# Where two DRAM sums of the down weights are formed, and the order of work at the change from up to down, in an encoder block on one core

## Chip, cores and metric

The kernel runs on one core of one Trainium2 chip. The metric is the device time of one execution in microseconds; the time before is the median of three runs. Names of engines: PE is TensorE, DVE is VectorE, ACT is ScalarE, POOL is GpSimd, SP is SyncE, which here only issues transfers.

## What is computed

One layer of an encoder: 512 positions, 1024 features, 4096 hidden features, all in float32. Cut to its outline:

```python
n = rms_norm(h, norm_mix_pre)
z_gmlp, q, k, v, gates = split(n @ w_in)                 # 1024 x 7680
y_a = gmlp_spatial_gating(gelu(z_gmlp), ...)             # 512 wide
y_b = dilated window attention of q, k, v                # 512 wide
g_a, g_b = sigmoid(gates + b_gate)
merged = g_a * (y_a @ w_branch_a) + g_b * (y_b @ w_branch_b)
h = h + rms_norm(merged @ w_out, norm_mix_post)
n2 = rms_norm(h, norm_mlp_pre)
hid = square(relu(n2 @ w_up))                            # 1024 -> 4096
h = h + rms_norm(hid @ w_down, norm_mlp_post)            # 4096 -> 1024
```

The change touches the gates (in one place), the product with `w_up`, called up here, and the product with `w_down`, called down.

## The kernel before

Every float32 operand of a matmul is split in two parts, a high one (a copy by ScalarE into the matmul's format) and a low one (VectorE subtracts the high part from the operand), and each product is three matmuls: high by high, high by low, low by high. So for each operand that TensorE reads, ScalarE and VectorE have one operation each, one after the other.

The stages follow each other: norm and projections, attention, the gMLP branch, the gates with the two branch products, `w_out`, up, down.

**Gates** (`seven_pairs`, `gate_weights`, `gate_evac`, `branches`). Seven groups i = 0 to 6 of 256 gate columns. Each loads 1 MB of `w_in` into tile `gw` (two transfers on SP) and the branch weights `bw`, forms sums of quarter blocks on VectorE (line 331 is the first), splits them and runs seven half-size products of Strassen's kind (line 345) and the branch products (lines 84 to 86, tile `pf`).

**Up** (line 1000 on). The first four tiles of 128 hidden columns are plain products. Then i runs from 2 to 15, a group being 256 hidden columns. `prep` loads 1 MB of `w_up` into tile `upw` (`raw_up`, line 930, pool `wback`, tag `raw`, two buffers), forms four sums (line 970 is the first) and splits them; the high and low parts `hl` share five buffers. Seven products follow, numbered 6, 1, 5, 2, 7, 3 and 4 in the order of the code (line 995), 12 matmuls each. Product 4 of a group stands in `tail`, which is called in the next group behind product 6; its join (line 1035) and the Relu of the pair (line 1037) follow, and the Square (line 1018) in the next group. The first half of the second column tile, `c1`, is ready after product 2 (line 1023).

**Down** (line 1040 on). The 4096 hidden features are four groups c = 0 to 3 of 1024 (`hid`), and the product is one level of Strassen's scheme with seven products, each over four groups: X with activations a11, Z with a12, Y with a21, W with a12 plus a sum, X again with s2, Z with a11 plus a sum, Y with a22. A group of a product (`run`, lines 1081 to 1083, tile `pd`) is 24 matmuls of 128 by 512 columns, with one split of its activations (`h_split`, tile `hhl`) and two splits of its weights (`w_split`, tile `hl`). The weights of the first, second and fourth product come straight from `w_down` (`block`, line 1057, tile `dnw`, the same two `raw` buffers as up's loads). The other three need sums of weight blocks:

- `t1d` in DRAM, for the sixth product: two blocks added, read at line 1062.
- `t3d` in DRAM, for the third product: two blocks added; line 1116 loads it into SBUF (`tsum`, and `tend` for the last group), and `add_block` (line 1111) then adds further blocks in place for the fifth and the seventh product.

Both DRAM sums are formed by transfers from DRAM to DRAM on POOL's queue (`form_next`, line 736): per sum and group c a copy of 1 MB, then an accumulating transfer of 1 MB, which waits until its copy has landed. The list `forming` gives the order. `form_next` ties a transfer to a place in the program by a one-element copy on POOL out of a tile that was just written; what is issued after it follows in POOL's order. Whoever writes that tile again waits for this copy: in up that is the Relu of the same pair.

**What sets the order.** The code order is only a start: a scheduler moves instructions on each engine, and `tc.issue_after(x)` holds what stands under it behind x. The engines then run their lists in order. SP's list holds all loads of weights, so a load that waits for its buffer holds those behind it. In down, `h_split` is held behind `late`, two results of the last group but one of up; the weight splits are not held.

Of the kernel before, what the change touches and what calls it, by code (L numbers as in the profile page):

```python
# [10 lines left out]
F32 = mybir.dt.float32  # L11
F32R = mybir.dt.float32r
AF = mybir.ActivationFunctionType
ALU = mybir.AluOpType
# [22 lines left out]
def block_kernel(ctx: ExitStack, tc: tile.TileContext, x, norm_mix_pre, w_in, b_gate, ln_v_gain, ln_v_bias,  # L37
# [40 lines left out]
    def split_into(hi, lo, src, sub=nc.vector):  # L78
        nc.scalar.activation(hi, src, AF.Copy)  # L79
        return sub.tensor_tensor(lo, src, hi.bitcast(F32), op=ALU.subtract)  # L80
# [610 lines left out]
    for g2 in range(2):  # L691
        raw = wload([KD, 2 * P], lambda r: [(r, fcols(w_in, COL_U + g2 * 2 * P, KD, 2 * P))], "uw")
        for j in range(2):
# [15 lines left out]
            for c in range(4):  # L709
# [19 lines left out]
    w7 = w_down.rearrange("(c j h p) d -> c h p j d", p=P, h=2, j=4)  # L729
    halves = [slice(0, 512), slice(512, 1024)]  # L730
    t1d, t3d = [tc.dram_tile([4, P, 4, 512], F32, name=nm) for nm in ("t1d", "t3d")]
    forming = [(t, c, *part) for t, parts in ((t1d, ((0, 0, None), (0, 1, ALU.add))), (t3d, ((0, 1, None), (1, 1, ALU.add))))
               for c in range(4) for part in parts]

    def form_next(seen, n=1):
        ins = nc.gpsimd.tensor_copy(warm[:1, :1], seen)
        with tc.issue_after(ins.ins):
            for _ in range(n):
                t, c, h, hf, op = forming.pop(0)
                nc.gpsimd.dma_start(t[c], w7[c, h, :, :, halves[hf]], **({"accum_op": op} if op else {}))  # L740
# [22 lines left out]
    def gate_evac(i, dst, X):  # L763
        d = i + GSTD
        nc.scalar.activation(dst, X, AF.Sigmoid, bias=cols[:, d:d + 1])
        if i < 6:
            form_next(dst[:1, :1], 2 if i < 2 else 1)

    def gate_after(i):
        d = i + GSTD  # L770
# [220 lines left out]
    def product(n, ps, w, first):  # L991
        (wh, wl), (bh, bl) = w[n], moving[n]
        for j in range(KH):
            for m, (a, b) in enumerate(((wh, bh), (wh, bl), (wl, bh))):
                nc.tensor.matmul(ps, a[:, j], b[:, j], start=first and not (j or m), stop=(j == KH - 1 and m == 2), skip_group_check=True)  # L995

    def half_bank(tag):
        return psB.tile([P, 512], F32, name="p" + tag, tag=tag, bufs=4)[:, :256]
# [5 lines left out]
    for i in range(NSTD, KF // 2):  # L1004
        f = 2 * i
        if f % 8 == 0:
            hid.append((hida if f < 24 else hidb).tile([P, 8, S], F32, name="hid"))
        c2, c1 = hid_of(f), hid_of(f + 1)
        w = prep(i)
        Y, Z, X = half_bank("acc"), half_bank("acc"), half_bank("tp")  # L1010
        product(6, Y, w, True)
        both = tail()[1] if tail else None
        product(1, X, w, True)
        p1, z5, u2, u3 = snap("p1", 2), snap("z5"), snap("u2"), snap("u3")
        taken = nc.scalar.activation(p1, X, AF.Copy)
        if both is not None:
            with tc.issue_after(taken.ins):
                nc.scalar.activation(both, both, AF.Square)
        joins[i] = nc.vector.tensor_tensor(u2, Y, p1, op=ALU.add)
        product(5, Z, w, True)  # L1020
        nc.scalar.activation(z5, Z, AF.Copy)
        product(2, X, w, False)
        done = nc.scalar.activation(c1[:, :256], X, AF.Copy)
        if i > NSTD + 1 and forming:
            form_next(c1[:1, :1])
        product(7, Y, w, False)
        nc.vector.scalar_tensor_tensor(u3, Y, -1.0, p1, op0=ALU.mult, op1=ALU.subtract)
        product(3, Z, w, False)
        nc.vector.tensor_tensor(c1[:, 256:], Z, u2, op=ALU.add)
        ins = nc.vector.tensor_tensor(c2[:, 256:], u3, z5, op=ALU.subtract)  # L1030
        late = late if i == KF // 2 - 1 else (done, ins)

        def tail(w=w, Y=Y, p1=p1, c2=c2, f=f):
            product(4, Y, w, False)
            joined = nc.vector.scalar_tensor_tensor(c2[:, :256], Y, -1.0, p1, op0=ALU.mult, op1=ALU.subtract)
            both = hid[f // 8][:, f % 8:f % 8 + 2]
            nc.scalar.activation(both, both, AF.Relu)
            return joined, both
    joined, both = tail()
    up.close()  # L1040

    dpool = pool(dn, "dpool", bufs=3)
# [11 lines left out]

    def block(c, h, hf):
        raw = raw_down()
        nc.sync.dma_start(raw, w7[c, h, :, :, halves[hf]])
        return raw

    def formed(c):  # L1060
        raw = raw_down()
# [6 lines left out]
    def h_split(src, first=False):  # L1068
        hl = (d0pool if first else dpool).tile([P, 2, 4, 256], F32R, name="hhl", tag="hhl")
        with tc.issue_after(late[0].ins), tc.issue_after(late[1].ins):  # L1070
            lows.append(split_into(hl[:, 0], hl[:, 1], src))
        return hl[:, 0], hl[:, 1]

    lows = []

    def w_split(parts):
        return [split_back(part, [2, 512]) for part in parts]
# [16 lines left out]
    a11, a12, a21, a22 = [[b[:, :, h, z * 256:z * 256 + 256] for b in blk] for z in range(2) for h in range(2)]  # L1094

    for c in range(NC):
        run(X, c, True, h_split(a11[c], c == 0), w_split(pairs(block(c, 0, 0))))
        if c == 1:
            nc.scalar.activation(both, both, AF.Square)
    big = sumpool.tile([P, 4 * NC - 4, 512], F32, name="tsum")  # L1100
# [10 lines left out]
            nc.gpsimd.dma_start(part, w7[c, h, :, js, halves[hf]], accum_op=ALU.add)  # L1111

    s2 = []
    for c in range(NC):
        for part, js in each_part(c):
            nc.sync.dma_start(part, t3d[c, :, js])

    def first_sums(c, after):
        with tc.issue_after(after.ins):
# [5 lines left out]
    first_sums(1, lows[3])  # L1125
    for c in range(NC):
        run(Z, c, True, h_split(a12[c]), w_split(pairs(block(c, 1, 0))))
        if c in (1, 2):
            first_sums(c + 1, lows[-1])

# [129 lines left out]
```

## Time and profile before

| | us |
|---|---|
| three runs | 1096.55, 788.82, 791.18 |
| their median | 791.18 |
| the profiled execution | 794.81 |
| its span, from the first to the last instruction | 793.0 |
| TensorE busy in the span | 775.2 |
| VectorE, ScalarE, GpSimd busy | 603.0, 461.4, 92.4 |
| mean granted TensorE clock in the span | 0.993 |
| transfers: SP's queue, POOL's queue | 83.50 MB, 43.61 MB |

The page's times are of the one profiled execution, in us from the first instruction; a group's row gives the line, the engine, the operation, tiles written and read, size, count, busy time and the mean of one in ns. A wait is put down to what ended it. In this execution the gates run from about 297 to 418, `w_out` to 477, up to 633, down to the end.

### The profile page before, as it was taken

What the parts mean: (1) busy time and instruction counts of PE and PEld (TensorE: products, weight loads), DVE (VectorE), ACT (ScalarE), POOL (GpSimd) and SP (SyncE); (2) the same over time, 40 slices, a digit from 0 to 9 for tenths busy, and PEclk for the clock granted to TensorE, in tenths of its full rate; (3) what the DMA queues carried; (4) which work ended last, traced back from release to release, by engine and by line L of the source; (5) the groups of instructions that cost most, each with busy time, mean ns of one, the idle gap of its engine ahead of it and who ended that gap; (6) DMA issues with size and microseconds to landing.
All of it is one profiled execution on the core that took longest, in us unless ns stands there. A gap on an engine that the chain in (4) does not pass through costs nothing.

```text
span 793.0 us, 12277 instructions
## 1 busy us (share of the span) xinstructions
PE 775.2 (98%) x4821; PEld 696.6 (88%) x4821; DVE 603.0 (76%) x963; ACT 461.4 (58%) x747; POOL 92.4 (12%) x125
## 2 busy tenths in 40 slices
PE   9999999999999999979999999999999989999996
PEld 6888999999988889979998899999999868888885
DVE  6884688979665977758756569998888688968885
ACT  6351467978776454435444557566666565665671
POOL 2310200010105200100110210001110000202010
PEclk9999999999999999989999999999999999999999
DMA  9733734353616324877674521449873774979802
GB/s 311 237 113 115 204 100 107 86 155 104 189 53 180 99 80 118 229 186 164 204 205 133 197 102 59 157 131 243 214 210 112 264 289 163 181 236 206 227 0 107
DMA packets 104748, 128.29 MB, mean 162 GB/s; under 512 B 3265, under 2 KB 75233, under 8 KB 103794
## 3 DMA queue, kind: packets, MB, share of 16 engines
q1 hardware_dynamic: 83920, 83.50, 33.4%
q0 software_dynamic: 20480, 43.61, 23.0%
q8 instruction: 38, 0.62, 0.3%
q10 hardware_dynamic: 290, 0.40, 0.1%
q14 instruction: 20, 0.16, 0.1%
HBM read 117.53 MB, written 26.74 MB: 182 GB/s over the span
## 4 chain that ended last, share of the span: by engine, by line
PE 88%; DMA 5%; DVE 3%; ACT 2%; issue 1%; POOL 0%; SPq 0%; POOLq 0%; DVEq 0%; ACTq 0%
PE pacc L995 10%; PE pg L345 10%; PE pd L1081 6%; PE pd L1083 6%; PE pd L1082 6%; PE pgacc L345 6%; PE pf L86 5%; PE pf L85 5%; PE pf L84 5%; PE ptp L995 4%; PE pv L84 3%; PE pv L85 3%; PE pv L86 3%; PE pgS L345 2%; PE pd L84 2%; PE pd L86 2%
## 5 line engine op out<-in xcount | busy, mean ns | idle before, releaser
L1081 PE MATMUL pd<-hl,hhl 128*128 128x512 f32 x224 | 87.5, 392 | 4.5 <-ACT hhl L79 4.5
L1082 PE MATMUL pd<-hl,hhl 128*128 128x512 f32 x224 | 87.9, 392 | 0.0
L1083 PE MATMUL pd<-hl,hhl 128*128 128x512 f32 x224 | 87.4, 392 | 0.0
L995 PE MATMUL pacc<-nt,hl 128*128 128x256 f32 x504 | 67.1, 280 | 0.0
L995 PEld LDWEIGHTS pacc<-nt,hl 128*128 128x128 f32 x504 | 62.6, 188 | 0.1
L1081 PEld LDWEIGHTS pd<-hl,hhl 128*128 128x128 f32 x224 | 42.4, 190 | 13.4 <-ACT hhl L79 4.8
L74 ACT ACTIVATE hi<-s 128x1024 fp32r<-128x1024 f32 x30 | 31.7, 1059 | 36.7 <-DVE s L332 13.4
L1083 PEld LDWEIGHTS pd<-hl,hhl 128*128 128x128 f32 x224 | 42.4, 189 | 9.0
L1082 PEld LDWEIGHTS pd<-hl,hhl 128*128 128x128 f32 x224 | 42.3, 189 | 8.9
L80 DVE TENSOR_TENSOR hl<-dnw,hl 128x1024 fp32r<-128x1024 f32 x32 | 38.5, 1221 | 9.6 <-ACT hl L79 9.6
L75 DVE TENSOR_TENSOR lo<-s,hi 128x1024 fp32r<-128x1024 f32 x30 | 36.6, 1223 | 11.1 <-ACT hi L74 11.0
L79 ACT ACTIVATE hl<-s 128x1024 fp32r<-128x1024 f32 x28 | 29.4, 1058 | 26.8 <-DVE s L978 18.2
L995 PE MATMUL pacc<-n,hl 128*128 128x256 f32 x336 | 44.8, 279 | 0.0
L79 ACT ACTIVATE hl<-dnw 128x1024 fp32r<-128x1024 f32 x32 | 33.7, 1057 | 19.0 <-PE pd L1083 9.1
L84 PE MATMUL pf<-nh,hi 128*128 128x512 f32 x112 | 44.3, 396 | 0.0
L86 PE MATMUL pf<-nh,lo 128*128 128x512 f32 x112 | 44.1, 393 | 0.0
L85 PE MATMUL pf<-nl,hi 128*128 128x512 f32 x112 | 44.0, 393 | 0.0
L995 PEld LDWEIGHTS pacc<-n,hl 128*128 128x128 f32 x336 | 41.9, 188 | 0.1
L79 ACT ACTIVATE hhl<-hid 128x1024 fp32r<-128x1024 f32 x24 | 25.3, 1058 | 25.1 <-PE pd L1083 25.0
L80 DVE TENSOR_TENSOR hhl<-hid,hhl 128x1024 fp32r<-128x1024 f32 x24 | 29.3, 1222 | 13.6 <-ACT hhl L79 13.3
L80 DVE TENSOR_TENSOR hl<-s,hl 128x1024 fp32r<-128x1024 f32 x28 | 34.2, 1222 | 6.2 <-ACT hl L79 6.1
L85 PE MATMUL pv<-lo,nh 128*128 128x512 f32 x96 | 37.6, 392 | 0.0
(383 smaller groups left out, 2278.5 us busy)
## 6 DMA issues: line engine op xcount, KB each, us to landing
upw<-in_w_up_dram SPq DMA_DIRECT2D x16, 1024.0 KB, 5.6
qkw<-in_w_in_dram SPq DMA_DIRECT2D x24, 512.0 KB, 5.2
dnw<-in_w_down_dram SPq DMA_DIRECT2D x12, 1024.0 KB, 5.3
gw<-in_w_in_dram SPq DMA_DIRECT2D x16, 512.0 KB, 5.8
t1d<-in_w_down_dram POOLq DMA_DIRECT2D x8, 1024.0 KB, 9.0
t3d<-in_w_down_dram POOLq DMA_DIRECT2D x8, 1024.0 KB, 9.1
slab<-in_w_in_dram SPq DMA_DIRECT2D x6, 1024.0 KB, 10.2
tsum<-in_w_down_dram POOLq DMA_DIRECT2D x6, 1024.0 KB, 9.5
```

The lines of the kernel that those rows point to most:

```text
L74: nc.scalar.activation(hi, raw, AF.Copy)
L75: (sub or nc.vector).tensor_tensor(lo, raw, hi.bitcast(F32), op=ALU.subtract)
L79: nc.scalar.activation(hi, src, AF.Copy)
L80: return sub.tensor_tensor(lo, src, hi.bitcast(F32), op=ALU.subtract)
L84: nc.tensor.matmul(ps, ah, bh, start=start, stop=False)
L85: nc.tensor.matmul(ps, ah, bl, start=False, stop=False)
L86: return nc.tensor.matmul(ps, al, bh, start=False, stop=stop)
L345: nc.tensor.matmul(ps, a[:, j], b[:, j], start=first and not (j or i), stop=(j == KH - 1 and i == 2), skip_group_check=True)
L995: nc.tensor.matmul(ps, a[:, j], b[:, j], start=first and not (j or m), stop=(j == KH - 1 and m == 2), skip_group_check=True)
L1081: nc.tensor.matmul(ps, ah, bh, start=start, stop=False, skip_group_check=True)
L1082: nc.tensor.matmul(ps, ah, bl, start=False, stop=False, skip_group_check=True)
L1083: return nc.tensor.matmul(ps, al, bh, start=False, stop=stop, skip_group_check=True)
```

## The change

Four things:

1. `forming` is turned round: t3d first, then t1d. In the gates nothing is formed any more. In up, groups 4 to 15 form all 16 transfers, two each in groups 6, 8, 10 and 12, one in the others. Before, the gates' first six groups formed the eight for t1d (2, 2, 1, 1, 1, 1) and groups 4 to 11 of up the eight for t3d.
2. The first down product's first group is held behind the last matmul of up's last product (`turned`).
3. In the first down product, the load and the weight splits of groups 2 and 3 are held behind both operations of the activations' split of the same group; `h_split` is written out for this, with its two operations in lists.
4. The loads of t3d into SBUF stand one behind each weight load of the second product, instead of ahead of that product.

```diff
-    forming = [(t, c, *part) for t, parts in ((t1d, ((0, 0, None), (0, 1, ALU.add))), (t3d, ((0, 1, None), (1, 1, ALU.add))))
+    forming = [(t, c, *part) for t, parts in ((t3d, ((0, 1, None), (1, 1, ALU.add))), (t1d, ((0, 0, None), (0, 1, ALU.add))))
                for c in range(4) for part in parts]
...
         nc.scalar.activation(dst, X, AF.Sigmoid, bias=cols[:, d:d + 1])
-        if i < 6:
-            form_next(dst[:1, :1], 2 if i < 2 else 1)
...
-                nc.tensor.matmul(ps, a[:, j], b[:, j], start=first and not (j or m), stop=(j == KH - 1 and m == 2), skip_group_check=True)
+                ins = nc.tensor.matmul(ps, a[:, j], b[:, j], start=first and not (j or m), stop=(j == KH - 1 and m == 2), skip_group_check=True)
+        return ins
...
-        if i > NSTD + 1 and forming:
-            form_next(c1[:1, :1])
+        if i > NSTD + 1:
+            form_next(c1[:1, :1], 2 if i in (6, 8, 10, 12) else 1)
...
-            product(4, Y, w, False)
+            turned = product(4, Y, w, False)
...
-            return joined, both
-    joined, both = tail()
+            return joined, both, turned
+    joined, both, turned = tail()
...
-        nc.sync.dma_start(raw, w7[c, h, :, :, halves[hf]])
+        loads.append(nc.sync.dma_start(raw, w7[c, h, :, :, halves[hf]]))
...
-            lows.append(split_into(hl[:, 0], hl[:, 1], src))
+            his.append(nc.scalar.activation(hl[:, 0], src, AF.Copy))
+            lows.append(nc.vector.tensor_tensor(hl[:, 1], src, hl[:, 0].bitcast(F32), op=ALU.subtract))
...
     for c in range(NC):
-        run(X, c, True, h_split(a11[c], c == 0), w_split(pairs(block(c, 0, 0))))
+        h = h_split(a11[c], c == 0)
+        with ExitStack() as order:
+            if c > 1:
+                order.enter_context(tc.issue_after(his[-1].ins))
+                order.enter_context(tc.issue_after(lows[-1].ins))
+            w = w_split(pairs(block(c, 0, 0)))
+        with nullcontext() if c else tc.issue_after(turned.ins):
+            run(X, c, True, h, w)
...
-    for c in range(NC):
-        for part, js in each_part(c):
-            nc.sync.dma_start(part, t3d[c, :, js])
...
         run(Z, c, True, h_split(a12[c]), w_split(pairs(block(c, 1, 0))))
+        for part, js in each_part(c):
+            with tc.issue_after(loads[-1].ins):
+                nc.sync.dma_start(part, t3d[c, :, js])
```

What this makes of the engines' lists is shown at three places. ScalarE where up ends: `p`, `z` and `hid` out of PSUM are up's last group, line 1037 is the Relu of the last pair and line 1099 its Square; `hl<-dnw` are weight splits of the first down product, two per group, `hhl<-hid` its activation splits. Before:

```order
L1021 ACTIVATE z_6836<-pacc 128x256
L79 ACTIVATE hl<-dnw 128x1024
L1018 ACTIVATE hid<-hid 128x1024
L79 ACTIVATE hl<-dnw 128x1024
L1023 ACTIVATE hid<-ptp 128x256
L79 ACTIVATE hl<-dnw 128x1024 x3
L1037 ACTIVATE hid<-hid 128x1024
L79 ACTIVATE hhl<-hid 128x1024 x2
L1099 ACTIVATE hid<-hid 128x1024
```

Now (lines 1020, 1017, 1022, 1036 and 1108 are the old 1021, 1018, 1023, 1037 and 1099; 1072 is the activation split's own line):

```order
L1020 ACTIVATE z_6832<-pacc 128x256
L79 ACTIVATE hl<-dnw 128x1024
L1017 ACTIVATE hid<-hid 128x1024
L1022 ACTIVATE hid<-ptp 128x256
L79 ACTIVATE hl<-dnw 128x1024
L1036 ACTIVATE hid<-hid 128x1024
L1072 ACTIVATE hhl<-hid 128x1024 x2
L79 ACTIVATE hl<-dnw 128x1024
L1108 ACTIVATE hid<-hid 128x1024
```

The three weight splits ahead of the Relu, the last of which is the fourth group's, have become one, the second group's; the others stand behind the activations. On TensorE, in the same stretch, 14 of the first group's 24 matmuls `pd` stood between up's products 5 and 2 and ten more ahead of product 4; now all 24 stand behind product 4, in one piece, and up's products 5, 2, 3, 7 and 4 follow each other directly.

POOL in up, `hid` being the tile that was just written; before, the last two of eight triggers:

```order
L736 COPY warm<-hid 1x1
L740 DMA t3d<-in_w_down_dram 512x1x512
L736 COPY warm<-hid 1x1
L740 DMA t3d<-in_w_down_dram 512x1x512
L1045 DMA gain_6918<-in_norm_mlp_post_dram 128x1024
```

Now, from the seventh trigger (group 10) on:

```order
L736 COPY warm<-hid 1x1
L740 DMA t1d<-in_w_down_dram 512x1x512 x2
L736 COPY warm<-hid 1x1
L740 DMA t1d<-in_w_down_dram 512x1x512
L736 COPY warm<-hid 1x1
L740 DMA t1d<-in_w_down_dram 512x1x512 x2
L736 COPY warm<-hid 1x1
L740 DMA t1d<-in_w_down_dram 512x1x512
L736 COPY warm<-hid 1x1
L740 DMA t1d<-in_w_down_dram 512x1x512
L1044 DMA gain_6916<-in_norm_mlp_post_dram 128x1024
L736 COPY warm<-hid 1x1
```

Each one-element copy now stands behind up to two transfers of the group before, and the last one behind the load of the norm's gain.

SP at the start of down, before:

```order
L1057 DMA dnw<-in_w_down_dram 128x4x512 x2
L1116 DMA tend<-t3d 128x1024
L1057 DMA dnw<-in_w_down_dram 128x4x512
L1116 DMA tend<-t3d 128x1024
L1057 DMA dnw<-in_w_down_dram 128x4x512
L1116 DMA tsum<-t3d 128x2048 x3
L1057 DMA dnw<-in_w_down_dram 128x4x512 x8
```

Now:

```order
L1056 DMA dnw<-in_w_down_dram 128x4x512 x5
L1136 DMA tsum<-t3d 128x2048
L1056 DMA dnw<-in_w_down_dram 128x4x512
L1136 DMA tsum<-t3d 128x2048
L1056 DMA dnw<-in_w_down_dram 128x4x512
L1136 DMA tsum<-t3d 128x2048
L1056 DMA dnw<-in_w_down_dram 128x4x512
L1136 DMA tend<-t3d 128x1024 x2
L1056 DMA dnw<-in_w_down_dram 128x4x512 x4
```

The five loads of t3d, which stood among and behind the first product's weight loads, each follow a weight load of the second product.

More of the change, by code (lines that the diff above doesn't have):

```diff
@@ L1056, in block @@
         raw = raw_down()
-        nc.sync.dma_start(raw, w7[c, h, :, :, halves[hf]])
+        loads.append(nc.sync.dma_start(raw, w7[c, h, :, :, halves[hf]]))
         return raw
+    loads = []
     def formed(c):
@@ L1070, in h_split @@
         with tc.issue_after(late[0].ins), tc.issue_after(late[1].ins):
-            lows.append(split_into(hl[:, 0], hl[:, 1], src))
+            his.append(nc.scalar.activation(hl[:, 0], src, AF.Copy))
+            lows.append(nc.vector.tensor_tensor(hl[:, 1], src, hl[:, 0].bitcast(F32), op=ALU.subtract))
         return hl[:, 0], hl[:, 1]
-    lows = []
+    his, lows = [], []
     def w_split(parts):
```

## The prediction

> **What bounds the kernel now.** I read the page's first part, then TensorE's waits, then stretches around each wait.
>
> ```profile
> PE 775.2 (98%) x4821; PEld 696.6 (88%) x4821; DVE 603.0 (76%) x963; ACT 461.4 (58%) x747; POOL 92.4 (12%) x125
> ```
> ```profile
> PE pd L1081 <- ACT hhl L79: 4.5, 1, 4.5
> PE pgacc L345 <- DVE u L365: 4.0, 1, 4.0
> ```
>
> TensorE is the bound: of the 793.0 us span it is idle in 17.8. So whatever the change does to transfers or to other engines counts only where it makes or ends an idle stretch of TensorE. Two waits in the middle make up nearly half of the idle time. In the stretches below the columns are length, busy time (instructions) of TensorE, of its weight loads, of VectorE, ScalarE and GpSimd, then granted clock, DMA share, GB/s.
>
> ```profile
> 348.65:352.69 4.04, 0.01 (x1) 0.01 (x1) 2.22 (x4) 0.00 (x0) 0.00 (x0) 0.83 0.58 193
> 352.69:358.16 5.47, 5.47 (x21) 5.08 (x22) 5.21 (x10) 3.96 (x6) 0.00 (x0) 0.50 0.00 0
> 633.23:637.78 4.55, 0.00 (x1) 0.01 (x1) 2.54 (x4) 3.01 (x4) 0.00 (x0) 1.00 1.02 424
> 638.06:641.47 3.41, 3.41 (x9) 2.62 (x9) 3.41 (x4) 2.62 (x3) 0.00 (x0) 0.50 1.00 409
> 0.00:20.00 20.00, 18.15 (x61) 12.97 (x62) 12.83 (x25) 12.92 (x29) 5.48 (x15) 1.00 0.94 312
> 780.00:793.00 13.00, 6.53 (x29) 5.07 (x27) 4.48 (x9) 1.37 (x4) 1.10 (x2) 0.95 0.29 105
> ```
>
> After each of the two waits the granted clock is 0.50: for 5.47 us of matmuls behind the first, for 3.41 behind the second. Half of that is lost as well: 2.7 and 1.7. So the wait in the gate stage costs 4.0 + 2.7 = 6.8, the wait between up and down 4.55 + 1.7 = 6.3. The other idle time is the start (1.85) and the tail (6.5), which the change does not touch.
>
> The **gate wait**, from the chain that ended last, the issues, and the page's median for such a load:
>
> ```profile
> 337.37 12.98 DMA gw<-in_w_in_dram
> 350.47 1.23 DVE s L331
> 352.69 2.93 PE pgacc L345 x12
> ```
> ```profile
> 335.24 1.18 POOL L740 DMA_DIRECT2D t1d<-in_w_down_dram  x1 [7.19 <-DMA t1d<-in_w_down_dram]
> 336.96 1.65 SPq L66 DMA_DIRECT2D gw<-in_w_in_dram  x2
> 342.50 0.67 POOL L740 DMA_DIRECT2D t1d<-in_w_down_dram  x1
> ```
> ```profile
> gw<-in_w_in_dram SPq DMA_DIRECT2D x16, 512.0 KB, 5.8
> ```
>
> A gate group's weights took 13.0 us to land where 5.8 is the median, between an accumulating transfer into t1d and the next copy. VectorE stood at its first sum until 350.47, and the join that frees TensorE's bank is queued behind that sum.
>
> The **wait between up and down**, by the timeline and the chain:
>
> ```profile
> 631.67 1.56 PE L995 MATMUL pacc<-n,hl 128*128 128x256 f32 x12
> 634.10 0.42 DVE L1035 SCALAR_TENSOR_TENSOR hid<-pacc,p 128x256 f32<-128x256 f32 x1
> 634.77 1.06 ACT L79 ACTIVATE hl<-dnw 128x1024 fp32r<-128x1024 f32 x1 [1.85 <-DMA dnw<-in_w_down_dram]
> 635.74 1.04 ACT L1037 ACTIVATE hid<-hid 128x1024 f32<-128x1024 f32 x1
> 636.68 1.04 ACT L79 ACTIVATE hhl<-hid 128x1024 fp32r<-128x1024 f32 x1
> 637.78 0.58 PE L1081 MATMUL pd<-hl,hhl 128*128 128x512 f32 x1 [4.55 <-ACT hhl L79]
> ```
> ```profile
> 627.26 7.43 DMA dnw<-in_w_down_dram
> ```
>
> Up's last product ends at 633.2. The second group's activations can be split only after its join and the Relu, and these stood behind a weight split for the fourth group, which waited for a load issued at 627.26. Meanwhile TensorE had nothing left: the first group's 24 matmuls had been run between up's last products.
>
> **The change, part by part.** Gates: eight transfers leave POOL's queue; what was late falls to the usual load time. Counted from the issue at 336.96, 5.8 us gives 342.8 instead of 350.35, and TensorE ran dry only at 348.65. Take away 6.8. Nothing else is removed there: each dropped one-element copy ran on POOL, which is 12% busy.
>
> Junction: the first group's matmuls now stand behind up's last one. Their price in TensorE's time is zero; they fill the hole. Pace of both kinds, from full stretches:
>
> ```profile
> L80 DVE TENSOR_TENSOR hhl<-hid,hhl 128x1024 fp32r<-128x1024 f32 x24 | 29.3, 1222 | 13.6 <-ACT hhl L79 13.3
> ```
> ```profile
> 660.00:680.00 20.00, 20.00 (x90) 16.57 (x89) 17.62 (x17) 12.05 (x13) 2.61 (x2) 1.00 0.60 162
> 600.00:620.00 20.00, 20.00 (x172) 20.00 (x172) 16.18 (x22) 13.63 (x19) 0.00 (x0) 1.00 0.31 106
> ```
>
> 20/90 gives 0.22 us per down matmul, 24 of them 5.3. So up ends 5.3 earlier, at 627.9, and the second group is wanted at 633.2. Its chain after 627.9: join 0.42 and Relu 1.04, high half 1.04, low half 1.22 (mean of such a subtraction), with some 0.5 of handing over: ready at 632.1 to 632.5. That fits by about 0.9. The third and fourth groups' weight splits now stand behind their activations, so no load holds ScalarE ahead of the Relu. Take away 6.3; if the 0.9 is overdrawn, some tenths come back, without a clock loss.
>
> Everything after it comes 4.6 to 6.3 us earlier, and then loads are late next. The second product's first load goes out when the third group's second weight split is done: six operations of 1.22 stand on VectorE from 631.2 on, so 638.5. It is wanted three groups after 633.2, at 649.1, and 2.3 before for its own split: it may take 8.3 us.
>
> ```profile
> 628.17 1.36 SPq L1116 DMA_DIRECT2D tsum<-t3d  x3
> ```
> ```profile
> tsum<-t3d SPq DMA_DIRECT2D x3, 1024.0 KB, 11.7
> ```
> ```profile
> DMA to landing us min/median/max: 4.8/6.0/11.1
> DMA to landing us min/median/max: 5.4/5.6/9.6
> DMA to landing us min/median/max: 3.9/5.8/13.0
> ```
>
> The last three are the landings of the tiles dnw, upw and gw, in this order. The 11.1 was the load behind the three t3d transfers, which now follow it on SP; but a t1d transfer may still run beside it. Between 6.0 (no cost) and 11.1 (2.7, plus 1.7 of clock at worst) I take 1, nearer to the median since the three are gone. The t3d transfers, now put one behind each load of the second product, go out from 639 to 656; at 11.7 each they are there by 668, and the third product wants them from 633.2 + 8 x 5.3 = 676 on: nothing.
>
> Up: eight more forming transfers in the same twelve groups, POOL's queue twice blocked per pair. The present load of this stage:
>
> ```profile
> 527.00:597.00 70.00, 70.00 (x597) 70.00 (x596) 60.09 (x86) 46.01 (x66) 11.45 (x14) 1.00 0.86 218
> ```
> ```profile
> L740 POOL DMA_DIRECT2D t3d<-in_w_down_dram x8: 645/806/1203, 510.9 to 587.6; - x8
> L1062 SPq DMA_DIRECT2D dnw<-t1d x4: 319/329/339, 705.5 to 742.7; - x4
> ```
> ```profile
> 583.99 0.37 SPq L930 DMA_DIRECT2D upw<-in_w_up_dram  x1
> 595.51 1.22 DVE L970 TENSOR_TENSOR s<-upw 128x1024 f32<-128x1024 f32 x1
> 603.97 10.08 SPq L1057 DMA_DIRECT2D dnw<-in_w_down_dram  x2
> 545.95 0.40 POOL L736 COPY warm<-hid 1x1 f32<-1x1 f32 x1 [7.32 <-ACT hid L1023]
> 552.93 1.04 ACT L1037 ACTIVATE hid<-hid 128x1024 f32<-128x1024 f32 x1
> ```
>
> From 600 to 620 two loads (603.97 and the next) at share 0.31 are 3.1 us of all DMA engines each. In 70 us at 0.86 are seven forming transfers (all but the first) and about seven loads: (60 - 22)/7 = 5.4 each. From the third trigger to the end of up, some 90 us, there will be 13 of them and nine loads: 70 + 28 = 98. So the queue is full, and the forming runs some 8 us behind. Its own readers don't mind: t3d, formed first, is read from 639 on, t1d from 705.5. A load does: it is used 11.5 us after its issue (583.99 to 595.51), so up to 11.5 costs nothing. The worst load of this stage, 9.6, already stood between two forming transfers. I take 0; the upper bound, at gw's 13.0, is (13.0 - 11.5)/2 x 10 groups = 7.5, since each buffer serves every second group. A gain is excluded, TensorE being full there.
>
> [...]
>
> POOL's queue: an accumulating transfer waits for its copy, and the next group's one-element copy stands behind it. The Relu (L1037) waits for that copy: 552.93 against 545.95, 7 us of room. POOL's waits before a second transfer were up to 7.19; a full DMA queue adds a few. I take 0; above it, ScalarE's delays of some 3 us, four times, 12 at the most if none is absorbed.
>
> **Sum.** 793.0 - 6.8 - 6.3 + 1 = 780.9 of span. The profiled execution took 794.8, so 782.7 by its clock; it is 3.6 above the median of the runs shown, 791.18, and part of its waits may be its own. On the median I take off 11.7: **779.5**.
>
> **Rivals.** (1) The wait between up and down only moves: the second product's first loads come late, since all groups start 5 us earlier. For it: 11.1 us for one of them, the last t1d transfer beside it. Against: t3d is behind them on SP. 2.7 for each of two groups and 1.7 of clock instead of my 1: 786.
>
> (2) Slower: up's loads starve. The sixteen transfers keep the queue full from the third trigger on, and every load takes more than 11.5 us. Each us beyond costs 0.5 per group, 5 in ten groups. The gain is used up from 13.9 us on; at 15.5 a load the cost is 20 us: 799.5. For it: 98 us of work for 90, gw's 13.0. Against: 9.6 as the longest in this stage, and such a load used half-KB rows and shared its queue with three others.
>
> (3) POOL's blocked queue holds the Relu four times: 12 us, 791.5, no change. For it: 7.19 against 7 us of room. Against: only that one of POOL's waits was as long, and only what goes beyond the 7 holds ScalarE.
>
> (4) The gate change does nothing: gw was late because it was itself issued late, at 336.96. Then 6.8 stay: 786.3. Against: 13.0 from issue to landing is counted after the issue.
>
> [...]
>
> **How the numbers follow.** The forecast has 0.60, rival (1) 0.17, (2) 0.10, (3) 0.05, (4) 0.08. Its own spread, with the scatter of the runs, is 775 to 784. To leave out no more than two in ten, the range goes over (1), (4) and part of (3): **774 to 790**. Two per cent, about what a measurement of this kernel can tell from no change, is 15.8 us. The waits that can go are worth 13.1, so faster by more than that needs luck in the runs: 0.10. Slower by more than that needs loads beyond 17 us: 0.04. Within: 0.86.
>
> **What would show it.** Right: no wait of TensorE at L345 in the gates and granted clock 1.00 there; gw landing below 8; pd's first 24 matmuls in one piece, a wait before the 25th below 1 us; TensorE full through up with DMA share near 1; upw landing at 7 to 10. Wrong: a wait of TensorE in up on VectorE's sums or ScalarE's splits (rivals 2 and 3), the Relu held by POOL's copy, or a wait on hl or hhl around the second product's first groups (rival 1). The sum is wrong if the total of TensorE's idle time is not 9 to 11 us.

## The result, and the profile after

The changed kernel takes 782.17 us (median of nine runs, 780.58 to 786.94), the kernel before beside it 791.54: ratio 0.9896, 95% interval 0.9867 to 0.9925. It is about 1% faster: the interval does not reach 1, and the change stays inside the two per cent that the prediction held most likely. The ratio is taken over the executions and not from the two medians, whose quotient is 0.988; one execution of the kernel before, at 1096.55, was in a slower state and is left out of it. The forecast was 779.5 in a range of 774 to 790. The profiled execution took 782.17 with a span of 780.3; before it was 793.0.

The page's first part, of the changed kernel:

```profile
PE 771.0 (99%) x4821; PEld 693.4 (89%) x4821; DVE 602.5 (77%) x963; ACT 460.6 (59%) x747; POOL 90.8 (12%) x123
```

TensorE is idle in 780.3 - 771.0 = 9.3 us of the span, where it was 17.8. Its waits, all of the changed kernel:

```profile
PE idle L159 <- DVE onesq L59: 1.1, 1, 1.1
PE pt L186 <- DVE xn L182: 0.7, 1, 0.7
PE pacc L993 <- DVE u L1026: 0.5, 1, 0.5
PE pd L84 <- DVE gs L372: 0.5, 1, 0.5
PE ptp L993 <- ACT hl L79: 0.2, 1, 0.2
```

Both long waits are gone, the one at L345 in the gates and the one on `hhl` between up and down. A small one is new: up's last product (4) now runs directly behind product 7, on the same PSUM bank, and waits 0.5 for the join that reads it. Stretches of the changed kernel, columns as before (gates, up, the junction):

```profile
337.00:353.00 16.00, 16.00 (x115) 15.02 (x114) 12.79 (x21) 7.97 (x14) 0.00 (x0) 1.00 0.43 112
527.00:597.00 70.00, 70.00 (x597) 70.00 (x596) 59.54 (x87) 46.04 (x65) 14.63 (x18) 1.00 0.95 255
620.00:634.00 14.00, 14.00 (x68) 11.79 (x68) 10.83 (x11) 9.88 (x11) 1.19 (x1) 1.00 1.06 306
```

The granted clock is 1.00 in all three, TensorE is busy throughout, and up's DMA share went from 0.86 to 0.95. What ScalarE does at the junction, in the changed kernel:

```profile
622.03 1.06 ACT L1036 ACTIVATE hid<-hid 128x1024 f32<-128x1024 f32 x1 [1.69 <-DVE hid L1034]
623.00 1.99 ACT L1072 ACTIVATE hhl<-hid 128x1024 fp32r<-128x1024 f32 x2
627.30 1.06 ACT L79 ACTIVATE hl<-dnw 128x1024 fp32r<-128x1024 f32 x1 [2.31 <-DMA dnw<-in_w_down_dram]
```

The Relu (L1036) now waits only for its own join. The third group's weight split still waits 2.31 for its load, but behind the activations, where nobody needs it yet. The landings of the tiles upw and dnw, in this order, in the changed kernel:

```profile
DMA to landing us min/median/max: 5.4/5.6/12.0
DMA to landing us min/median/max: 4.7/7.4/13.5
```

Both maxima rose (9.6 and 11.1 before). The loads did get later; in this execution TensorE did not wait for them.

### The profile page after: what moved, and what is told of

It reads as the page before. It is cut to its first block, busy times and chain, and to the rows that moved or that the text cites. A ratio compares the mean times of both kernels' runs of the same rounds, so it can differ in the third digit from the quotient of the medians.

```text
span 780.3 us, 12276 instructions
## 1 busy us (share of the span) xinstructions
PE 771.0 (99%) x4821; PEld 693.4 (89%) x4821; DVE 602.5 (77%) x963; ACT 460.6 (59%) x747; POOL 90.8 (12%) x123
## 4 chain that ended last, share of the span: by engine, by line
PE 95%; DMA 2%; ACT 1%; issue 0%; DVE 0%; POOL 0%; POOLq 0%; DVEq 0%; ACTq 0%
PE pacc L993 11%; PE pg L345 10%; PE pd L1083 6%; PE pd L1084 6%; PE pd L1085 6%; PE pgacc L345 6%; PE pf L85 5%; PE pf L84 5%; PE pf L86 5%; PE ptp L993 5%; PE pv L84 4%; PE pv L86 4%; PE pv L85 4%; PE pgS L345 3%; PE pd L84 2%; PE pd L86 2%
## 5 line engine op out<-in xcount | busy, mean ns | idle before, releaser
L1084 PE MATMUL pd<-hl,hhl 128*128 128x512 f32 x224 | 87.1, 389 | 0.0
L1085 PE MATMUL pd<-hl,hhl 128*128 128x512 f32 x224 | 87.0, 389 | 0.0
L1083 PE MATMUL pd<-hl,hhl 128*128 128x512 f32 x224 | 85.3, 390 | 0.0
L86 PE MATMUL pv<-hi,nl 128*128 128x512 f32 x96 | 37.3, 392 | 0.0
L84 PE MATMUL pv<-hi,nh 128*128 128x512 f32 x96 | 36.9, 392 | 0.0
```

The lines of the kernel that those rows point to most:

```text
L84: nc.tensor.matmul(ps, ah, bh, start=start, stop=False)
L86: return nc.tensor.matmul(ps, al, bh, start=False, stop=stop)
L1083: nc.tensor.matmul(ps, ah, bh, start=start, stop=False, skip_group_check=True)
L1084: nc.tensor.matmul(ps, ah, bl, start=False, stop=False, skip_group_check=True)
L1085: return nc.tensor.matmul(ps, al, bh, start=False, stop=stop, skip_group_check=True)
```

## Experiments

Twelve kernels ran, the changed one twice. The table gives each one's median and its ratio to the kernel before in the same job (kernels that ran side by side). "Parts" are the four points of the section on the change: 1 the forming in up alone, 2 the first group behind up, 3 the weight loads and splits behind the activations, 4 the loads of t3d behind those of the second product.

| kernel | parts | median us | ratio, 95% interval |
|---|---|---|---|
| changed | 1 2 3 4 | 782.17 | 0.9896 (0.9867 to 0.9925) |
| changed, again | 1 2 3 4 | 781.90 | 0.9880 (0.9834 to 0.9926) |
| forming only | 1 | 796.4 | 1.0059 (1.0035 to 1.0082) |
| forming put back | 2 3 4 | 785.35 | 0.9912 (0.9879 to 0.9945) |
| junction only | 2 3 | 786.32 | 0.9902 (0.9866 to 0.9939) |
| first group free | 1 3 4 | 784.97 | 0.9914 (0.9881 to 0.9947) |
| splits free | 1 2 4 | 788.37 | 0.9950 (0.9926 to 0.9973) |
| t3d loads first | 1 2 3 | 794.87 | 1.0036 (1.0015 to 1.0058) |
| no t1d | 1 2 3 4, half of the forming | 781.10 | 0.9854 (0.9824 to 0.9884) |
| one each | 2 3 4, forming spread | 780.64 | 0.9845 (0.9815 to 0.9874) |
| one each, turned | the same, product order | 780.31 | 0.9830 (0.9798 to 0.9863) |
| extra copies, tied to nothing | 1 2 3 4, 12 MB more at the start | 788.95 | 0.9958 (0.9933 to 0.9983) |
| extra copies in up | 1 2 3 4, 12 MB more | 807.71 | 1.0182 (1.0144 to 1.0220) |

The medians of the kernel before in the four jobs were 791.5, 791.7, 792.5 and 794.4, so kernels of different jobs are compared by ratio.

### Forming alone

The kernel before with part 1 alone:

```diff
-    forming = [... t1d ..., ... t3d ...]
+    forming = [... t3d ..., ... t1d ...]
...
-        if i < 6:
-            form_next(dst[:1, :1], 2 if i < 2 else 1)
...
-        if i > NSTD + 1 and forming:
-            form_next(c1[:1, :1])
+        if i > NSTD + 1:
+            form_next(c1[:1, :1], 2 if i in (6, 8, 10, 12) else 1)
```

> The kernel before with the forming alone moved (t3d first, all 16 transfers in up, none in the gates); the order at the end of up and the t3d loads are as before. Theory A (two separate waits: t1d's transfers delay a gate load, the order of work delays the second down group): the gate wait is gone with its clock loss, 4.0 + 2.7 = 6.8 us, and the wait behind up stays at 4.5 us or grows, since the down loads now run beside the last t1d transfers: 785 us, ratio 0.991. Rival B (the gate load was late because it was issued late): the gate wait stays, 791, ratio 1.00. Rival C (forming all 16 in up takes back what the gates give): gate wait gone, waits of TensorE in up, 788 to 792.

It came out slower than before, ratio 1.0059. TensorE's longest wait in it, the stretch of that wait and the one behind it, and ScalarE's rows ahead of the Relu (L1035):

```profile
PE pd L1079 <- ACT hhl L79: 12.9, 1, 12.9
```
```profile
624.77:637.67 12.90, 0.01 (x1) 0.00 (x0) 3.94 (x5) 5.00 (x6) 1.19 (x1) 0.61 1.04 357
637.67:651.32 13.65, 13.65 (x53) 11.11 (x54) 12.66 (x11) 7.80 (x8) 0.00 (x0) 0.87 0.83 270
```
```profile
628.56 2.00 ACT L79 ACTIVATE hl<-dnw 128x1024 fp32r<-128x1024 f32 x2 [9.86 <-DMA dnw<-in_w_down_dram]
634.67 1.06 ACT L79 ACTIVATE hl<-dnw 128x1024 fp32r<-128x1024 f32 x1 [4.11 <-DMA dnw<-in_w_down_dram]
635.63 1.04 ACT L1035 ACTIVATE hid<-hid 128x1024 f32<-128x1024 f32 x1
```

The gate wait is gone, but the wait between up and down grew from 4.55 to 12.9, with 13.65 x (1 - 0.87) = 1.8 of clock behind it. ScalarE stood 9.86 and 4.11 us in weight splits ahead of the Relu, waiting for loads that now run beside t1d's transfers. So part 1 moves the contention from the gates to the junction, and the junction as it was cannot stand it. None of the three theories had the time: theory A allowed that the wait grows, but not by more than the gates give.

### Forming put back, and the junction alone

The changed kernel with part 1 undone (the diff above, reversed), and the kernel before with parts 2 and 3 alone:

> The changed kernel with the forming put back (t1d in the gates, t3d in up), the rest as changed. Theory A: the gate wait of 4.0 us and its clock loss are as before, the wait behind up is gone: 791.5 - 6.3 = 785 us, ratio 0.992, and no t1d transfer beside the first down loads. Rival C: with up free of the moved transfers this one is as fast as the whole change or faster, below 782.

> The kernel before with parts 2 and 3 of the change alone (first group behind up, weight loads and splits of groups 2 and 3 held behind the activations): forming as before, loads of t3d ahead of the second product as before. In SP's list the fourth group's load then stands behind all five loads of t3d, 4 MB at 3.1 us each. Theory A (the 12.7 us by which the changed kernel lost when these loads were put first again come from SP's order alone): 788 to 794, with a wait of 3 to 9 us on the fourth group's weights. Theory B (they come from that order together with t1d transfers that run beside it, which this kernel has not): the fourth load lands by 635 to 637 where it is wanted at 635, a wait of at most 2: 784 to 788.

They took 785.35 (ratio 0.9912) and 786.32 (0.9902): the junction's order is worth 7 to 8 us without any change of the forming. These are the times of theory A for the first and of theory B for the second. In both, the wait between up and down is gone and the gate wait is back. TensorE's wait there, and the gate load in the chain that ended last, first with the forming put back, then with the junction alone:

```profile
PE pgacc L345 <- DVE u L365: 2.6, 1, 2.6
```
```profile
336.89 11.55 DMA gw<-in_w_in_dram
```
```profile
PE pgacc L345 <- DVE u L365: 4.9, 1, 4.9
```
```profile
336.42 13.85 DMA gw<-in_w_in_dram
```

With the kernel before, whose load took 12.98 for a wait of 4.04, that makes three executions of one and the same program text in the gates. Landing less wait is 11.55 - 2.62, 12.98 - 4.04 and 13.85 - 4.92: each time 8.9. The load has 8.9 us of room, and each us beyond is a us of TensorE's wait. How far beyond differs by execution. The clock behind the waits, with the forming put back and with the junction alone:

```profile
350.77:356.00 5.23, 5.23 (x40) 5.05 (x41) 5.23 (x10) 3.80 (x7) 0.00 (x0) 1.00 0.02 6
```
```profile
352.61:360.00 7.39, 7.39 (x45) 7.11 (x46) 7.39 (x14) 5.24 (x9) 0.00 (x0) 0.77 0.20 59
```

Behind 2.62 of waiting the clock stayed at 1.00; behind 4.92 it was 0.77 over 7.39 us, 1.7 lost. So the gate wait costs 2.6, 6.8 and 6.6 in these three, and the profile of before had caught the dearest.

The junction alone has the loads of t3d in their old place, and no wait on the fourth group's weights; the experiment on the loads of t3d comes back to this.

### The first group free, the splits free

The changed kernel without part 2, and without part 3's holds:

```diff
-        with nullcontext() if c else tc.issue_after(turned.ins):
-            run(X, c, True, h, w)
+        run(X, c, True, h, w)
```

> The changed kernel without the hold on the first down group, so its 24 matmuls run between up's last products again; the weight splits stay behind the activations. Theory A (the first group's matmuls are the cover for join, Relu and activation split): TensorE waits behind up's last product for join 0.4 + Relu 1.0 + high half 1.0 and handing over, about 3.4 us against 4.55 before, plus 1.7 of clock: 5 us slower than the whole change, 787, ratio 0.996. Rival D (what counted was the fourth group's weight split ahead of the Relu): no wait, 782, ratio 0.99.

```diff
-        with ExitStack() as order:
-            if c > 1:
-                order.enter_context(tc.issue_after(his[-1].ins))
-                order.enter_context(tc.issue_after(lows[-1].ins))
-            w = w_split(pairs(block(c, 0, 0)))
+        w = w_split(pairs(block(c, 0, 0)))
```

> The changed kernel without holding the third and fourth groups' weight splits behind the activations; one more weight split (the third group's) then stands ahead of the Relu. Theory A: that split costs ScalarE 1.06 us ahead of the Relu, against 0.9 us of room in the cover: a wait of TensorE below 1 us, 782 to 783, ratio 0.99. Rival D: the wait behind up comes back with 4 us and the clock loss, 787 to 788, ratio 0.996.

They took 784.97 (0.9914) and 788.37 (0.9950). With the first group free, TensorE's wait, the stretch behind it, and the half-speed stretch, which begins only 1.4 us behind the wait:

```profile
PE pd L1083 <- ACT hhl L1072: 2.6, 1, 2.6
```
```profile
628.77:632.18 3.41, 3.34 (x9) 2.40 (x10) 3.41 (x4) 3.41 (x4) 0.00 (x0) 0.71 1.12 240
630.17:633.59 3.42, 3.42 (x9) 2.65 (x10) 3.42 (x4) 3.39 (x5) 0.00 (x0) 0.50 1.12 210
```

That is 2.61 of waiting and 3.42 x 0.50 = 1.7 of clock: the chain from up's last product to the second group, no longer covered by 24 matmuls. It is what theory A said, with a shorter wait than its 3.4. In the medians the loss is smaller, 0.9914 against 0.9896 and 0.9880, and those intervals overlap. With the splits free, the wait and ScalarE's row that made it, with the Relu behind:

```profile
PE pd L1083 <- ACT hhl L1072: 5.1, 1, 5.1
```
```profile
629.51 1.06 ACT L79 ACTIVATE hl<-dnw 128x1024 fp32r<-128x1024 f32 x1 [8.71 <-DMA dnw<-in_w_down_dram]
630.48 1.04 ACT L1036 ACTIVATE hid<-hid 128x1024 f32<-128x1024 f32 x1
```

One weight split ahead of the Relu is 1.06 us of work, and it cost 5.1 of waiting and some 2 of clock (0.69 granted over the next 6.83), because it waits 8.71 for its load and the Relu waits with it. This is rival D's time; theory A had priced the split and not its load. So part 3 is worth more than part 2, and its price is that of the load, not of the split.

### The loads of t3d first

The changed kernel without part 4:

```diff
+    for c in range(NC):
+        for part, js in each_part(c):
+            nc.sync.dma_start(part, t3d[c, :, js])
...
-        for part, js in each_part(c):
-            with tc.issue_after(loads[-1].ins):
-                nc.sync.dma_start(part, t3d[c, :, js])
```

> The changed kernel, with the loads of t3d into SBUF ahead of the second product again, as they were before. Theory A (the prediction's allowance): the second product's first loads then stand behind three of these loads and land in about 11 us instead of 5.6; each of the first two groups waits up to 2.7 us and the clock may drop: 784 to 786, with a wait of TensorE on hl or hhl near the end of the first product. Rival B: the wait is set at the junction alone and these loads have room: 782, no such wait, ratio to the changed kernel within 0.2%.

794.87, ratio 1.0036: undoing this one part costs the whole gain and more. TensorE's wait, SP's rows and ScalarE's row in it, and the landings of dnw:

```profile
PE pd L1083 <- ACT hl L79: 10.2, 2, 8.8
```
```profile
618.98 1.42 SPq L1125 DMA_DIRECT2D tsum<-t3d  x3
621.33 27.72 SPq L1056 DMA_DIRECT2D dnw<-in_w_down_dram  x3
```
```profile
645.21 2.00 ACT L79 ACTIVATE hl<-dnw 128x1024 fp32r<-128x1024 f32 x2 [6.61 <-DMA dnw<-in_w_down_dram]
```
```profile
DMA to landing us min/median/max: 4.8/6.9/23.9
```

Theory A's direction was right, but not its place or its size. The late load is not the second product's first but the first product's fourth: part 3 holds it behind the activations, so the scheduler puts it behind all five loads of t3d in SP's list, where it stood ahead of the last three before. It landed 23.9 us after its issue. The junction alone has the same list on SP, and no t1d transfers beside it. There the longest landing of dnw is this:

```profile
DMA to landing us min/median/max: 4.7/5.5/13.2
```

and TensorE does not wait: theory B of the kernel with the junction alone, although the load landed at 640.5 and not at its 635 to 637. So neither the order on SP nor the t1d transfers make the loss, only both together. Part 4 is needed because of parts 1 and 3.

### No t1d, one transfer each

The changed kernel without forming t1d (the sixth product reads a block of `w_down` in its place, so that sum is left out), and with one transfer per group, four in the gates' groups 2 to 5 and twelve in up:

```diff
+        if 2 <= i < 6:
+            form_next(dst[:1, :1])
...
-            form_next(c1[:1, :1], 2 if i in (6, 8, 10, 12) else 1)
+            form_next(c1[:1, :1])
```

> The changed kernel without the second sum: t1d is never formed, eight forming transfers in groups 4 to 11 of up instead of sixteen, and the sixth product reads a block of w_down where it read t1d (so that sum is left out of the result). Theory A: the full queue in up and the t1d transfers that run into down make the scatter of the changed kernel's executions (780.6 to 786.9 in nine) and its stalls there; without them the median falls by 2 to 4, to 778 to 780, with loads of up at 9.6 or less, and the first down loads at about 6. Rival B: the sixteen transfers cost nothing, as predicted: 781 to 783, and the scatter stays.

> The changed kernel with the sixteen transfers one per group: four in the gates' groups 2 to 5, twelve in up's groups 4 to 15. Theory A: what costs is a queue that is never empty; with one transfer per group nothing queues, up's loads stay below 9.6, forming ends inside up, and the down loads land at 6 to 8: 779 to 781. Rival B: any transfer beside a load of the gates makes TensorE wait there (4.0 before, 2.6 with all eight forming transfers put back), while up had no wait to lose: 783 to 786, with a wait at the gates' products of 1 to 4 us.

They took 781.10 (780.58 to 782.37) and 780.64 (779.75 to 781.06). The first has rival B's median, but its scatter is small, as theory A had it. The second took theory A's time without all of its signs: one load of up took 11.8, not below 9.6, and the last transfer landed at 627.6, some 8 us behind up's end. Landings of dnw, first without t1d, then with one transfer each:

```profile
DMA to landing us min/median/max: 4.9/5.7/10.6
```
```profile
DMA to landing us min/median/max: 4.8/6.5/9.5
```

Against 13.5 in the changed kernel the latest load comes at 9.5, and four transfers in the gates cause no wait there. The four are one to a group; before, two each had been triggered in the first two groups.

### The changed kernel again, and a better version

> The changed kernel itself, unaltered, for a second set of executions beside the other kernels of this job. Its executions scattered from 780.6 to 786.9 where the one without t1d took 780.6 to 782.4 and the one with one transfer per group 779.8 to 781.1. Theory A (queued forming transfers make some loads later than the 11.5 us that up leaves them, in some executions): 781 to 784, again with a scatter of 4 or more. Rival B (chance): a scatter below 2.

The changed kernel took 781.90, from 780.41 to 788.84: two of its six executions stood at 787 and 789, as three of nine had stood at 784.7 to 786.9 in the first job. The three kernels without t1d or with one transfer each showed no execution above 782.4 in sixteen. So theory A holds as far as scatter goes: the late executions come with sixteen transfers in up, four times two at once. Whether it is the pairs or the number was not told apart. Which load is late in them is open, since both profiles caught undisturbed executions.

The better version is the kernel with one transfer each, and product 7 of up's last group held ahead of product 3:

```diff
-        product(7, Y, w, False)
+        seventh = product(7, Y, w, False)
...
-        product(3, Z, w, False)
+        with tc.issue_after(seventh.ins) if i == KF // 2 - 1 else nullcontext():
+            product(3, Z, w, False)
```

> The kernel with one transfer per group (four in the gates' groups 2 to 5, twelve in up), and in up's last group product 7 held ahead of product 3, as in the other groups' code: the changed kernel runs 7 and then 4 on the same bank and TensorE waits 0.5 for the join between them. Theory A: that wait goes: 780.1, 0.5 below the kernel with one transfer per group, and 1.5 to 2.5 below the changed kernel beside it. Rival B: the wait moves to the next product or the second group's splits: no change from 780.6.

780.31 (779.44 to 781.15), ratio 0.9830, and 1.6 below the changed kernel's median in the same job. TensorE's waits in it:

```profile
PE idle L159 <- DVE onesq L59: 1.1, 1, 1.1
PE pt L186 <- DVE xn L182: 0.6, 1, 0.6
PE pd L84 <- DVE gs L372: 0.5, 1, 0.5
PE pv L84 <- ACT v L280: 0.3, 1, 0.3
```

The 0.5 in up is gone. That the median fell by 0.3 is less than two jobs can tell apart.

### Extra copies in up

Twelve more copies of 1 MB, to see whether the rivals on late loads and on POOL's queue could happen. The first try tied them to nothing:

```diff
+            nc.gpsimd.dma_start(spare[i % 4], w7[i % 4, 1, :, :, halves[0]])
```

> The changed kernel with one more copy of 1 MB from DRAM to DRAM in each of up's last twelve groups (into a scratch tile that nobody reads): some 65 us more of DMA work in the 90 us where the prediction counted 98. Theory A (the rivals on loads and on POOL's queue are real, and decided by the amount): loads of up then take 14 us or more and each us beyond 11.5 costs 0.5 per group, or the Relu is held by POOL's copy: 800 to 840, with waits of TensorE inside up on VectorE or ScalarE. Rival B: a load takes turns with the one other queue however much that holds: loads stay at 10 to 12, up has no wait, and only forming runs late, into down, where it costs 2 to 8 us at the junction and at t3d's first reader: 784 to 790.

788.95, within rival B's range and yet no evidence: the scheduler had put the copies at the program's start. The stretch from 20 to 60 us, in this kernel and in the changed one:

```profile
20.00:60.00 40.00, 39.47 (x178) 32.47 (x177) 30.03 (x37) 18.62 (x31) 15.35 (x22) 0.95 1.07 380
```
```profile
20.00:60.00 40.00, 40.00 (x186) 32.96 (x185) 33.29 (x40) 18.03 (x24) 9.73 (x16) 1.00 0.56 178
```

The DMA share is 1.07 there instead of 0.56. The second try put each copy behind the trigger's one-element copy:

```diff
                 nc.gpsimd.dma_start(t[c], w7[c, h, :, :, halves[hf]], **({"accum_op": op} if op else {}))
+            nc.gpsimd.dma_start(spare[c], w7[c, 1, :, :, halves[0]])
```

> The changed kernel with one more copy of 1 MB from DRAM to DRAM (into a scratch tile that nobody reads) behind each of up's twelve triggers, held there by the same one-element copy as the forming transfers; in the run before this one the scheduler had moved these copies to the program's start. POOL's queue then has 28 transfers of 5.4 us of DMA work, 151, and the loads 28, for the 90 us from the third trigger on. Theory A (the rivals on starving loads and on POOL's queue were real possibilities, kept off only by the amount): loads of up take 14 us or more, each us beyond 11.5 costs 0.5 per group, and the one-element copies hold the Relu: 800 to 840, with waits of TensorE inside up. Theory B (a load takes turns with one other queue, however much that holds): loads of up stay at 10 to 13, TensorE waits less than 3 in all of up, and what is late is the forming, which ends some 60 us later and slows the first down loads: 784 to 792.

807.71, ratio 1.0182: theory A. Waits, landings of upw, and up as a whole:

```profile
PE pacc L995 <- ACT hl L79: 8.9, 2, 4.6
PE pacc L995 <- DVE u L1028: 6.3, 3, 4.1
```
```profile
DMA to landing us min/median/max: 5.5/5.6/22.6
```
```profile
527.00:640.00 113.00, 98.37 (x782) 97.29 (x780) 74.58 (x108) 60.58 (x85) 24.67 (x34) 0.92 1.04 309
```

The loads of up whose landing is recorded here took 16.7, 9.1, 12.0, 18.1, 22.6 and 22.2. By the prediction's price, half of what is beyond 11.5, these are (5.2 + 0.5 + 6.6 + 11.1 + 10.7) / 2 = 17.1; TensorE's stalls on them are 4.1, 4.6, 1.7 and 4.3, together 14.7. The price holds in sum, though not load by load: the one of 22.6 made the 1.7. What it lacked is the clock: TensorE is busy for 777.8 us in this kernel and for 771.0 in the changed one, with as many matmuls and a mean granted clock of 0.988 against 0.998, so 6.8 are lost to it. The Relu was not the late one: ScalarE waited for it 3.1 us in all of up, for the join each time.

## Why the prediction was right, and where not

**The span was right, and to within 0.6 us by luck.** 780.9 was forecast for the profiled execution, 780.3 came; the spans of the changed kernel's fifteen executions go from 778.6 to 787.1. Of the terms, the gate wait (6.8) and the wait between up and down (6.3) went as forecast; in place of the 1 us allowed for the second product's first loads stands another 0.5, that of product 4 behind 7. The rest of idle time, 9.3, lies in the 9 to 11 named.

**The step that failed is the one from the span to the median.** The prediction took nearly all of the profiled saving off the median of before (11.7), while noting that part of the profiled waits may be that execution's own. The medians differ by 9.4. The profiled execution of before stands 3.3 above its median and that of the changed kernel on it, so the profiled saving of 12.7 is 3.3 too much. That says how large the miss is, not where it lies; the runs point at two terms:

- The gate wait. 6.8 was one execution's; three executions show 2.6, 4.0 and 4.9 of waiting, with 0, 2.7 and 1.7 of clock; the mean is 5.3. The clock loss was counted as part of the wait, but it comes only sometimes.
- The sixteen transfers in up, whose price for up's loads the prediction put at nothing. The kernel with one transfer each has no gate wait either, and is at 0.9845 where the changed kernel is at 0.9896 and 0.9880: some 3 to 4 us, about half of them in the changed kernel's late executions. At which loads they arise, in up or at the junction, is open. Against the kernel with the forming put back, at 0.9912, the same 0.9845 makes the gate wait worth 5.3.

Undoing part 1 in the changed kernel costs only 1 to 3 us (0.9912 against 0.9896 and 0.9880), the one less the other. Of these ratios only 0.9912 and 0.9845 have intervals that do not overlap, so the split of the 3.3 is an estimate.

**The junction.** Up's last matmul ended at about 621.4, and the second group's activations were split by 625.3 (the two copies from 623.00, the subtraction behind). The 24 matmuls lasted until 626.8, so about 1.5 of room, where 0.9 was forecast. The wait of 0.5 ahead of product 4 cost no clock (1.00 granted from 620 to 634), as the prediction had it for some tenths. What the prediction did not see is how much hangs on the parts together. Part 4 had no term of its own: what it kept away was a late load of the second product, worth 4.4 us at worst in the sum, of which 1 was taken. Undone, it costs 11 to 12 us (1.0036 against 0.9896 and 0.9880). It took the landing of dnw from a trace without t1d transfers at the junction, although the change puts them there: they ran until 634.9, more than 13 us behind up's end, where some 8 had been estimated. The forecast came true because part 4 keeps SP's list free just there, which the prediction had seen only for the second product's loads.

**The second product's first loads** (rival 1). Their issue was forecast for 638.5 on the clock of before; less the 6.8 saved in the gates this is 631.7, and it was 631.92. The load landed in 5.6, so the wait did not move there: the allowance was not needed.

**Loads in up** (rival 2). Free up to 11.5 was right: loads of 12.0, and of 12.3 in the second profile, made no stall, and in the kernel with extra copies 16.7 did. The forecast of 7 to 10 was too narrow: the recorded loads beside the forming took 5.6 to 12.0, and the margin was used up. It was the author's estimate from the 9.6 that was the longest load of up before. The first load of up that the forming slowed took 11.8 with one transfer per group, 11.5 with the pairs and 16.7 with the extra copies; the recorded ones behind it took 5.6 to 8.0, 5.6 to 12.0 and 9.1 to 22.6. Even the 9.6 of before, which the prediction read as standing between two transfers, had both beside it for 2.7 us. How much POOL's queue holds does matter to a load on SP's queue: the longest of upw took 9.6 and 11.5 with eight forming transfers in up (before, no t1d), 11.8 with twelve (one each), 12.0, 12.3 and 12.4 with sixteen (the changed kernel twice, t3d loads first) and 22.6 with twelve copies more. The number of transfers alone does not give the time, and the reason is open.

**POOL's queue** (rival 3) never held the Relu; no run here showed that mechanism. **The gate change does nothing** (rival 4): wrong, since in the gates a load now lands in 6.0 at most and the wait is gone.

## What to carry to other kernels

Before a wait's price is taken from a profile, see whether it hangs on a transfer beside others: its length can differ by execution (here 2.6, 4.0 and 4.9 us), and the profiled one may be dear; the room a load has (here 8.9 us) is the steady number, the wait is what exceeds it. When background transfers are moved, look at the order of the loads in the new place as well: moving the forming loses alone (1.0059), does no harm with the order that it needs (0.9896 against 0.9912 without it), and gains clearly only when it is spread as well (0.9845), so each part's worth shows only with the others in place. One background transfer at a time, spread over more groups, beat pairs in fewer here, by a little in the median and by all of the late executions.

## What was not expected of the hardware

Landing less room gave the wait to within 0.01 us in three executions (8.93, 8.94, 8.93), so nothing else in that chain varied. And the clock does not follow the length of a wait alone: behind 2.62 us in the gates it stayed at 1.00, behind 2.61 at the junction it was 0.71 over the next 3.41. Nor did it fall at one place. In the gates of the kernel before it fell 2.69 us into the wait of 4.04, which began at 348.65, and stayed at 0.50 for 6.82:

```profile
351.34:358.16 6.82, 5.47 (x21) 5.09 (x22) 6.56 (x13) 3.96 (x6) 0.00 (x0) 0.50 0.01 3
```

Between up and down it fell 0.28 behind the end of the wait of 4.55 and stayed at 0.50 for 3.41; with the first group free it fell 1.4 behind the end of a wait of 2.61, for 3.42. What sets the moment is not shown here. So the price of a wait of 2.6 us can be 2.6 or 4.3.
